# The list scheduler's second pass run a second time, on its own result

## The chip, the cores and the metric

The kernel runs on one core of one Trainium2 chip. The metric is the device time of one execution in microseconds (us), from the first instruction to the last with what the runtime puts around them. TensorE, VectorE, ScalarE, GpSimd and SyncE are called PE, DVE, ACT, POOL and SP in the profile. All compute engines take their own list of instructions in order; SP's list is the queue that starts nearly all transfers.

## What is computed

One layer on a sequence of 1024 tokens, width 2048, all in float32. One input projection feeds a sparse attention (an indexer picks 256 keys for each query) and a Mamba-2 mixer; one output projection joins them, and a layer norm closes the layer.

```python
u = einsum('bsd,de->bse', x, w_in)
q, k, v, z_attn, q_idx, k_idx, w_idx, z_ssd, xbc, dt_raw = split(u)
# attention: rope on q, k, q_idx, k_idx; 8 query heads on 2 kv heads
score = sum_h relu(q_idx . k_idx) * w_idx      # admissible chunks only
sel = top_k(score, 256)
o_attn = softmax(q . k[sel]) @ v[sel] * silu(z_attn)
# mixer: causal conv, then a scan over chunks of 64 tokens
y = ssd(silu(conv(xbc)), softplus(dt_raw + bias), a_log) + d_skip * xs
o_ssd = rms_norm_by_group(y * silu(z_ssd)) * norm_w
out = layer_norm(alpha * x + concat(o_attn, o_ssd) @ w_out)
```

## The kernel before, in words

**Arithmetic.** A float32 product is made of three products of rounded halves: high·high, high·low, low·high. So every raw block of weights (wr, 128 x 1024) is rounded to its high part by ScalarE (wh) and the remainder is taken by VectorE (wl); inputs have halves xh and xl in the same way. The projections are done with a scheme of fewer block products, for which sums of weight blocks are formed first (wr<-wr,wr, mostly on VectorE, t_wacc in line 1264) and results are stored to and reloaded from scratch arrays in memory (u2, u3, t2, p1 and the like). PSUM banks are called pj (four, for projections), a (three) and o (one). A bank is drained by VectorE (u<-pj,u, t_comb in line 1118: add a scratch tile and store it in u). Some banks are preloaded by ScalarE before their matmuls (pj<-u, t_base in line 1097), with a tile u that SP loads from memory.

**Stages.** In order of time: the opening loads (to 14 us), the projections mixed with the indexer, the two top-k searches (ScalarE counts with u<-s,sm, VectorE steps in sm), the attention, and the mixer (t_ssd in line 2442: eight s<-s,ac and an exp s<-s for each piece, and softplus and exp that need another ScalarE table), up to 1374 us; then the rest of the output projection to 1566 us, and the layer norm's tail. t_turn (line 2337) transposes blocks by four SP transfers u<-u.

**Where the order comes from.** kernel() (line 2845) has the order made in three steps. First, Layer.run() writes a draft: each call of an engine is recorded as an Item by Engine (line 340), placed by a greedy simulation. Second, Order (line 370) takes the list of items and makes a new list. Third, Program.emit (line 603) issues the list; that is why every instruction of the profile has line 626.

Order works thus. link (line 397) finds for each item the earlier items that it depends on, by the list's order on each buffer and region, so the uses of a buffer keep their sequence. blocks (line 433) joins successive full matmuls of the list, as long as no newer result from outside is needed, into blocks that stay together. deadlines (line 466) goes through the list and gives each TensorE item as its due time the sum of the busy times of the TensorE items **ahead of it in the list**; then, backwards, each other item must be due early enough for those that need it:

```python
if x.key == "PE":
    x.due = t
    t += x.busy
...
took = self.transfer(x) + self.landing(x) + x.busy if x.dma else x.took
for j in x.after:
    y = self.items[j]
    x.due = min(x.due, y.due - took - self.gap(x, y))
```

A transfer counts its modelled length and its landing, with LATE = 2500 ns on top. run (line 529) then simulates the engines: TensorE takes the first block **in the list's order**, among the next 100, whose inputs have been there for 500 ns (next_block, line 512), or else the one that is ready soonest; each of the other queues takes, of the items that are ready, the one with the earliest due time. Eight lanes stand for transfers under way, and a change of ScalarE's table costs 1283 ns. The result is sorted by simulated start. Both the due times and TensorE's preference thus hang on the order of the list that comes in. In the kernel before, that is the draft's.

The function that the change touches:

## Time and profile before

| | |
|---|---|
| time, median of 3 runs | 1579.01 us (1578.07 to 1580.04) |
| the profiled execution's own time | 1579.93 us |
| its span, first to last instruction | 1578.1 us |
| granted TensorE clock | 0.997 |
| busy: PE / PEld / DVE / ACT / POOL | 1557.7 / 1302.0 / 1348.1 / 1026.3 / 221.9 us |
| transfers | 442.36 MB; queue q1 81.7% of 16 engines' span |

PE is TensorE's matmuls, PEld its loading of weights, which runs beside them. Names in the profile are those of tiles without their numbers: "pj<-xh,wh" is a matmul into a projection bank, "DMA wr<-wt" a load of raw weights. An idle time is given in brackets with what ended it. All instructions have line 626, so the tile names tell the step.

### The profile page before, as it was taken

Reading aid. Unit: us, or ns where it says so; the run is one execution under the profiler, and the core shown is the slowest. Engines: PE = TensorE matmul, PEld = TensorE weight load, DVE = VectorE, ACT = ScalarE, POOL = GpSimd, SP = SyncE. Lnnn points to the kernel's source line nnn. Section 1 sums busy time; section 2 is a strip of 40 time slices with the busy share of each in tenths; the row PEclk is TensorE's granted clock in tenths of the full one; section 3 lists DMA queues with packets and bytes.
Section 4 is the critical chain, followed back from the end, with each engine's and each line's share of the span. In section 5 each row is a group of like instructions: output and inputs, shape, how many; then the busy total and the mean of one; then the engine's idle time right before and its main releaser. Section 6 shows DMA issues by size and latency. Waiting matters only on the chain.

```text
span 1578.1 us, 24028 instructions
## 1 busy us (share of the span) xinstructions
PE 1557.7 (99%) x7677; PEld 1302.0 (82%) x7677; DVE 1348.1 (85%) x2499; ACT 1026.3 (65%) x1881; POOL 221.9 (14%) x219
## 2 busy tenths in 40 slices
PE   9999999999999999999999999999999999999997
PEld 7888898888888888888878888888878888788885
DVE  5989999997779897788968888997789777879996
ACT  5466676858996999777334575596877675733440
POOL 0000300011000010101312222163110002100200
PEclk9999999999999999999999999999999999999998
DMA  9558977899878886689879865877999999997653
GB/s 346 210 196 279 346 240 235 298 370 404 300 223 291 282 316 225 227 269 313 241 246 384 281 216 181 297 219 243 345 360 359 323 384 315 345 363 252 204 180 107
DMA packets 248766, 442.36 MB, mean 280 GB/s; under 512 B 52384, under 2 KB 107328, under 8 KB 248640
## 3 DMA queue, kind: packets, MB, share of 16 engines
q1 hardware_dynamic: 248128, 440.45, 81.7%
q8 instruction: 60, 0.98, 0.3%
q14 instruction: 66, 0.54, 0.1%
q10 hardware_dynamic: 512, 0.39, 0.1%
HBM read 319.23 MB, written 112.08 MB: 273 GB/s over the span
## 4 chain that ended last, share of the span: by engine, by line
PE 80%; DMA 10%; DVE 4%; SPq 3%; ACT 2%; issue 1%; POOL 0%; ACTq 0%; DVEq 0%; POOLq 0%
PE pj L626 64%; PE a L626 13%; PE o L626 3%; SPq L626 3%; DMA wr<-wt 2%; DVE u L626 2%; DMA zs<-u 1%; DMA u<-u 1%; DMA u<-o 1%; ACT s L626 1%; ACT u L626 1%; DMA u<-mx 1%; DVE wl L626 1%; DMA s<-arow 1%; DMA wr<-t 0%
## 5 line engine op out<-in xcount | busy, mean ns | idle before, releaser
L626 PE MATMUL pj<-xh,wh 128*128 128x512 f32 (+1 forms) x1496 | 576.9, 386 | 5.2 <-DVE u L626 3.2
L626 PE MATMUL pj<-xh,wl 128*128 128x512 f32 (+1 forms) x1496 | 570.2, 381 | 0.5 <-DVE wl L626 0.5
L626 PE MATMUL pj<-xl,wh 128*128 128x512 f32 (+1 forms) x1496 | 570.6, 382 | 0.0
L626 ACT ACTIVATE wh<-wr 128x1024 fp32r<-128x1024 f32 (+3 forms) x242 | 249.0, 1029 | 156.9 <-PE pj L626 115.2
L626 DVE TENSOR_TENSOR wl<-wr,wh 128x1024 fp32r<-128x1024 f32 (+3 forms) x239 | 293.1, 1227 | 46.1 <-ACT wh L626 42.7
L626 PEld LDWEIGHTS pj<-xh,wh 128*128 128x128 f32 x1496 | 281.6, 188 | 59.6 <-ACT pj L626 3.1
L626 PEld LDWEIGHTS pj<-xh,wl 128*128 128x128 f32 x1496 | 281.2, 188 | 55.1 <-DVE wl L626 1.3
L626 PEld LDWEIGHTS pj<-xl,wh 128*128 128x128 f32 x1496 | 281.6, 188 | 49.8 <-DVE xl L626 0.3
L626 DVE TENSOR_TENSOR u<-u,u 128x512 f32<-128x512 f32 (+8 forms) x242 | 157.4, 660 | 25.7 <-ACT u L626 14.6
L626 ACT ACTIVATE u<-u 128x512 f32<-128x512 f32 (+5 forms) x200 | 108.3, 553 | 104.3 <-DVE u L626 46.2
L626 PE MATMUL a<-u,u 128*128 128x512 f32 (+3 forms) x710 | 165.5, 343 | 0.7 <-DVE s L626 0.4
L626 PEld LDWEIGHTS a<-u,u 128*128 128x128 f32 x710 | 118.2, 189 | 20.8 <-DVE s L626 1.7
L626 ACT ACTIVATE u<-s,sm 128x896 bf16<-128x896 int16 (+7 forms) x132 | 129.0, 978 | 8.7 <-DVE sm L626 8.0
L626 PE MATMUL pj<-wh,xh 128*128 128x512 f32 x318 | 127.2, 401 | 0.0
L626 PE MATMUL pj<-wl,xh 128*128 128x512 f32 x318 | 124.3, 391 | 0.0
L626 PE MATMUL pj<-wh,xl 128*128 128x512 f32 x318 | 124.0, 391 | 0.0
L626 ACT ACTIVATE a<-a 128x512 f32<-128x512 f32 (+3 forms) x160 | 78.5, 504 | 58.2 <-PE a L626 50.1
L626 DVE TENSOR_TENSOR wr<-wr,wr 128x1024 f32<-128x1024 f32 (+1 forms) x78 | 95.9, 1231 | 8.4 <-DMA wr<-wt 5.8
L626 DVE TENSOR_TENSOR u<-pj,u 128x512 f32<-128x512 f32 (+1 forms) x109 | 72.2, 664 | 20.1 <-PE pj L626 18.2
L626 POOL TENSOR_SCALAR s<-s,sm 128x128 f32<-128x128 f32 (+7 forms) x64 | 64.0, 1013 | 135.8 <-DVE sm L626 116.4
L626 DVE SCALAR_TENSOR_TENSOR s<-a,wsc,s 128x512 f32<-128x512 f32 (+3 forms) x120 | 73.6, 644 | 4.5 <-ACT a L626 3.9
L626 DVE SCALAR_TENSOR_TENSOR u<-cv,cw,u 128x512 f32<-128x512 f32 x96 | 71.7, 762 | 2.4 <-ACT u L626 2.1
(289 smaller groups left out, 2161.7 us busy)
## 6 DMA issues: line engine op xcount, KB each, us to landing
wr<-wt SPq DMA_DIRECT2D x187, 512.0 KB, 5.5
u<-u SPq DMA_DIRECT2D x110, 256.0 KB, 5.2
wr<-t SPq DMA_DIRECT2D x44, 512.0 KB, 6.1
u<-wo SPq DMA_DIRECT2D x64, 256.0 KB, 4.1
ts<-u SPq DMA_DIRECT2D x64, 256.0 KB, 4.9
wr<-ts SPq DMA_DIRECT2D x32, 512.0 KB, 6.0
s<-xt SPq DMA_DIRECT2D x25, 512.0 KB, 6.4
wr<-wo SPq DMA_DIRECT2D x23, 512.0 KB, 6.2
```

The costliest lines, as they stand in the source:

```text
L626: getattr(engines[x.eng], x.op)(*[real(v) for v in x.args], **{k: real(v) for k, v in x.kw.items()})
```

## The change

The pass over the order is made twice: the second one takes the first one's result as its list. Nothing else is changed: the same items, costs, tiles and pools.

```diff
-        items = Order(layer.fl.sim, layer.fl.items).run()
+        items = layer.fl.items
+        for _ in range(2):
+            items = Order(layer.fl.sim, items).run()
```

In the second pass the due times are sums over the first pass's TensorE order, the blocks are cut from that order, and the preference of TensorE follows it. The set of instructions stays equal but for ScalarE's table loads (45, then 43). TensorE's order is the same up to about 30 us and from about 1374 us on; in between it differs in 44 pieces, and 1243 of 7427 steps change place. Three places:

SP's queue at 804 to 813 us, before. Names have a tile's number and that of its making; u_1514 is a transposing transfer (x4), wr_1501 and wr_1502 are the two weight blocks whose sum VectorE forms, u_1504 and u_1509 are scratch tiles, the u2, u3 and t2 are stores.

```order
L626 DMA u_1504_8525<-p1_1_6_6454 128x512
L626 DMA u3_1_4_8529<-u_1437_8057 128x512
L626 DMA u2_1_5_8537<-u_1484_8316 128x512
L626 DMA t2_1_6_8541<-wr_1433_8300 128x1024
L626 DMA u_1514_8550<-u_1513_8497 128x1x128 x4
L626 DMA wr_1501_8581<-wt 128x1024
L626 DMA wr_1502_8585<-wt 128x1024
L626 DMA u_1509_8591<-p1_1_7_6509 128x512
L626 DMA t2_1_7_8604<-wr_1463_8409 128x1024
L626 DMA u_1518_8609<-u_1517_8594 128x1x128 x4
```

The same place after:

```order
L626 DMA u_1504_8530<-p1_1_6_6444 128x512
L626 DMA u2_1_5_8539<-u_1484_8392 128x512
L626 DMA u_1498_8545<-u_1497_8438 128x1x128 x4
L626 DMA u3_1_4_8562<-u_1437_7950 128x512
L626 DMA wr_1501_8569<-wt 128x1024
L626 DMA wr_1502_8573<-wt 128x1024
L626 DMA u_1509_8580<-p1_1_7_6504 128x512
L626 DMA u_1514_8584<-u_1513_8535 128x1x128 x4
L626 DMA t2_1_7_8602<-wr_1463_8368 128x1024
L626 DMA wr_1503_8614<-wt 128x1024
L626 DMA u_1518_8624<-u_1517_8600 128x1x128 x4
```

The loads of wr_1501 and wr_1502 stand ahead of u_1514's four transfers, and behind those of u_1498; wr_1503 comes ahead of u_1518; t2_1_6 stands earlier, before this piece.

SP's queue at 1139 to 1147 us, before. u_2281 is the tile with which ScalarE preloads a bank; u_2259 to u_2261 feed the mixer's gate; wr_2275 and wr_2274 are weight blocks, mx a store.

```order
L626 DMA wr_2253_12276<-t2_1_5_8199 128x1024
L626 DMA u_2175_12298<-c0_3_10399 128x2x256
L626 DMA wr_2275_12304<-wt 128x1024
L626 DMA u_2259_12311<-z0_6_12231 128x512
L626 DMA u_2260_12319<-o0_3_11522 128x512
L626 DMA u_2281_12324<-u3_1_2_8185 128x512
L626 DMA u_2261_12335<-o0_3_11522 128x512
L626 DMA mx1_7_12344<-u_2188_11861 128x512
L626 DMA wr_2274_12353<-t2_1_6_8541 128x1024
```

After:

```order
L626 DMA wr_2253_12264<-t2_1_5_8189 128x1024
L626 DMA s4_2202_12281<-arow0_2758 128x2x512
L626 DMA u_2175_12287<-c0_3_10399 128x2x256
L626 DMA mx1_7_12295<-u_2188_11869 128x512
L626 DMA wr_2274_12305<-t2_1_6_8378 128x1024
L626 DMA u_2281_12310<-u3_1_2_8183 128x512
L626 DMA u_2259_12314<-z0_6_12243 128x512
L626 DMA u_2260_12328<-o0_3_11455 128x512
L626 DMA u_2261_12339<-o0_3_11455 128x512
L626 DMA wr_2275_12352<-wt 128x1024
```

u_2281 now stands ahead of u_2259, u_2260 and wr_2275, and behind mx1_7 and wr_2274. On ScalarE its preload goes ahead of all eight steps s<-s,ac of that piece instead of behind six of them.

ScalarE's queue at 1202 to 1211 us, before. pj_2397<-u_2394 preloads a bank; s4_2266 are the mixer's eight steps and its exp (128x1024); xh_2379 and xh_2366 are rounded inputs; u_2271 a product with a piece's row.

```order
L626 ACTIVATE xh_2379_12887<-u_2360_12819 128x512
L626 ACT_TABLE_LOAD
L626 ACTIVATE u_2271_12486<-s4_2266_12650 64x512
L626 ACTIVATE wh_2391_12910<-wr_2343_12740 128x1024
L626 ACTIVATE u_2271_12486<-s4_2266_12650 64x512
L626 ACTIVATE s4_2266_12650<-s4_2266_12650,ac1_933 128x128 x3
L626 ACTIVATE xh_2366_12941<-u_2357_12868 128x512
L626 ACTIVATE s4_2266_12650<-s4_2266_12650,ac1_933 128x128 x3
L626 ACTIVATE pj_2397_12960<-u_2394_12884 128x512
L626 ACTIVATE s4_2266_12650<-s4_2266_12650,ac1_933 128x128 x2
L626 ACTIVATE s4_2368_12572,sm_2414_12976<-a_2415_12969,eps_130 128x128 x2
L626 ACTIVATE s4_2266_12650<-s4_2266_12650 128x1024
```

After:

```order
L626 ACTIVATE xh_2362_12860<-u_2356_12780 128x512
L626 ACT_TABLE_LOAD
L626 ACTIVATE u_2271_12491<-s4_2266_12575 64x512 x2
L626 ACTIVATE wh_2391_12898<-wr_2343_12731 128x1024
L626 ACTIVATE s4_2266_12575<-s4_2266_12575,ac1_935 128x128 x7
L626 ACTIVATE xh_2366_12935<-u_2357_12866 128x512
L626 ACTIVATE s4_2266_12575<-s4_2266_12575,ac1_935 128x128
L626 ACTIVATE xh_2379_12944<-u_2360_12834 128x512
L626 ACTIVATE s4_2266_12575<-s4_2266_12575 128x1024
L626 ACTIVATE pj_2397_12966<-u_2394_12882 128x512
```

The preload of pj_2397 stands behind all eight steps, xh_2379 and the exp; xh_2379 stands behind xh_2366 instead of ahead of the table load.

## The prediction, made blind

> **What bounds the kernel now.** I read the engine totals first, then TensorE's busy time by stretch, then the list of its waits, and last the timeline around the largest of them. The totals of the page and the engine line of its chain of waits:
>
> ```profile
> PE 1557.7 (99%) x7677; PEld 1302.0 (82%) x7677; DVE 1348.1 (85%) x2499; ACT 1026.3 (65%) x1881; POOL 221.9 (14%) x219
> PE 80%; DMA 10%; DVE 4%; SPq 3%; ACT 2%; issue 1%; POOL 0%; ACTq 0%; DVEq 0%; POOLq 0%
> ```
>
> TensorE's busy time in four stretches; the columns are the stretch, its length, PE busy (instructions), granted clock, DMA share and GB/s:
>
> ```profile
> 0.00:14.00 14.00, 12.38 (x42) 1.00 0.78 246
> 14.00:1374.00 1360.00, 1352.23 (x6771) 1.00 0.84 289
> 1374.00:1566.00 192.00, 192.00 (x864) 1.00 0.69 232
> 1566.00:1578.10 12.10, 1.10 (x5) 0.64 0.49 141
> ```
>
> TensorE stands still for 1578.1 − 1557.71 = 20.4 us: 1.6 in the opening, 7.77 in the long middle, 0 in the output projection, 11.0 in the tail. The change leaves all work and its engines as they are, so it can win only idle time of TensorE. Its two orders are equal for TensorE up to about 30 us and from about 1374 us on, so opening, output projection and tail keep theirs: **at most 7.8 us (and what restarting costs) are to be had, all in the middle.** Nothing of the kind bounds a loss. Who ended the waits (us in total, times, longest):
>
> ```profile
> PE pj L626 <- DVE u L626: 3.2, 2, 1.9
> PE pj L626 <- ACT pj L626: 1.7, 2, 0.9
> PE o L626 <- DVE s L626: 0.6, 1, 0.6
> PE o L626 <- PE a L626: 0.5, 1, 0.5
> ```
>
> Six waits hold 6.0 of the 7.77 us. In the timeline of TensorE (start, length, instruction, idle before it):
>
> ```profile
> 721.40 0.47 PE L626 MATMUL pj<-xh,wh 128*128 128x512 f32 x1 [1.31 <-DVE u L626]
> 818.63 0.50 PE L626 MATMUL pj<-xh,wh 128*128 128x512 f32 x1 [1.87 <-DVE u L626]
> 1133.33 0.86 PE L626 MATMUL o<-s,u 128*128 128x256 f32 x5 [0.58 <-DVE s L626]
> 1153.92 0.50 PE L626 MATMUL pj<-xh,wh 128*128 128x512 f32 x1 [0.86 <-ACT pj L626]
> 1209.49 0.50 PE L626 MATMUL pj<-xh,wh 128*128 128x512 f32 x1 [0.89 <-ACT pj L626]
> 1351.81 1.09 PE L626 MATMUL o<-s,u 128*64 128x128 f32 x16 [0.51 <-PE a L626]
> ```
>
> Everywhere else TensorE takes up its next matmul without a gap, so a step of VectorE, ScalarE or a transfer that moves there costs nothing as long as it lands within the slack that the row of matmuls ahead gives it. The sum is therefore made over these six places, and then over the places that may become new ones.
>
> **The change part by part.** Counts of matmuls, vector instructions and transfers stay equal; the list falls from 45 to 43 ScalarE table loads. 1243 of the 7427 TensorE steps change place, by 77 at most, and so do 1575 of VectorE's 2379, 876 of ScalarE's 1546 and 738 of SP's 1468, mostly by one or two.
>
> *818.6 us.* SP's queue, then VectorE's, ahead of the longest wait:
>
> ```profile
> 806.54 4.04 SPq L626 DMA_DIRECT2D u<-u  x4
> 810.63 1.09 SPq L626 DMA_DIRECT2D wr<-wt  x2
> 813.09 0.69 DVE L626 TENSOR_TENSOR u<-u,u 128x512 fp32r<-128x512 f32 x1 [4.11 <-ACT u L626]
> 816.75 1.23 DVE L626 TENSOR_TENSOR wr<-wr,wr 128x1024 f32<-128x1024 f32 x1 [2.97 <-DMA wr<-wt]
> 817.89 1.28 DVE L626 TENSOR_TENSOR u<-pj,u 128x512 f32<-128x512 f32 x2
> ```
>
> The two weight loads stand behind four transpose transfers that hold SP for 4.04 us. VectorE then waits 2.97 us for them, sums them (1.23), and only then drains the PSUM bank (half of 1.28) that TensorE wants. In the new order those four transfers come behind the loads. Issued 4.0 us earlier, the loads have landed by about 812.7, when VectorE is free, and the drain no longer waits: −1.87. What was moved back, the four transfers, feeds a step of TensorE that itself stands 11 matmuls later. If u_1498's four, which now stand right ahead of the loads, hold them as long, 0.
>
> *721.4 us.* The last two of VectorE's steps before the wait ends:
>
> ```profile
> 719.43 1.22 DVE L626 TENSOR_TENSOR wl<-wr,wh 128x1024 fp32r<-128x1024 f32 x1
> 720.57 0.68 DVE L626 TENSOR_TENSOR u<-pj,u 128x512 f32<-128x512 f32 x1
> ```
>
> VectorE is working without a gap; the drain is late because it stands behind other work. The new order carries a weight sum into the piece ahead of the drain and small top-k steps out of it. A sum costs this much, if its data is there:
>
> ```profile
> L626 DVE TENSOR_TENSOR wr<-wr,wr 128x1024 f32<-128x1024 f32 x76 | 93.5, 1231 | 8.4 <-DMA wr<-wt 5.8 <-DMA wr<-t 2.5
> ```
>
> Bounds: −1.31 (wait gone), +0.8 (two thirds of a sum unhidden). I take −0.6, since several steps of the same size leave the piece.
>
> *1153.9 us.* TensorE waits for ScalarE's preload of a PSUM bank (pj<-u); ScalarE waits for that preload's own load, which SP issues last of these:
>
> ```profile
> 1143.36 0.32 SPq L626 DMA_DIRECT2D u<-z  x1
> 1144.41 0.32 SPq L626 DMA_DIRECT2D u<-o  x1
> 1144.79 0.42 SPq L626 DMA_DIRECT2D u<-u  x1
> 1153.27 0.60 ACT L626 ACTIVATE pj<-u 128x512 f32<-128x512 f32 x1 [1.03 <-DMA u<-u]
> ```
>
> Now that load precedes the u<-z and the two u<-o, and a weight load less and a store and another weight load more stand ahead of it; it can be issued about 1 us earlier. −0.86; 0 if DMA is too full (8.5 us pass here from issue to use).
>
> *1351.8 us.* A few hundred ns of VectorE work leave the chain that ends at it: −0.51, bound 0.
>
> *1209.5 us.* Another preload, with ScalarE's steps around it:
>
> ```profile
> 1202.36 0.63 ACT L626 ACTIVATE xh<-u 128x512 fp32r<-128x512 f32 x1 [1.35 <-DMA u<-mx]
> 1208.86 0.58 ACT L626 ACTIVATE pj<-u 128x512 f32<-128x512 f32 x1
> 1209.38 0.68 ACT L626 ACTIVATE s<-s,ac 128x128 f32<-128x128 f32 x2
> 1210.65 1.05 ACT L626 ACTIVATE s<-s 128x1024 f32<-128x1024 f32 x1
> ```
>
> The new order puts the preload behind the two small steps (0.68), the exp (1.05) and that xh (0.63): 2.36 later. The xh leaves its old place, with the 1.35 us that ScalarE waited there: 1.98 earlier. Net +0.4; bounds −0.3 (the earlier start counts, the exp moves past) and +2.0 (little of that start survives, as data of the steps between comes later).
>
> *1133.3 us.* A vector step s<-a,s that TensorE waits for:
>
> ```profile
> 1130.44 0.69 DVE L626 TENSOR_TENSOR u<-a,u 128x512 fp32r<-128x512 f32 x1 [2.26 <-DMA o<-u]
> 1132.58 0.69 DVE L626 TENSOR_TENSOR s<-a,s 128x512 fp32r<-128x512 f32 x1
> 1133.78 0.42 DVE L626 TENSOR_TENSOR u<-u,dt 128x256 f32<-128x256 f32 x1
> ```
>
> It goes behind the u<-u,dt (0.42) and a weight sum (1231 ns, the row above); part of the sum may fill the 2.26 us that VectorE stood still just before: +0.5, bounds −0.58 (wait gone) and +1.5 (nothing fills).
>
> Sum of the six: −1.87 − 0.6 − 0.86 − 0.51 + 0.4 + 0.5 = −2.9.
>
> *New waits.* Where 1243 matmul steps and their feeders trade places, TensorE will wait somewhere it does not now. No row prices that; the nearest is the old order's own yield, 7.77 us over 6771 matmuls. A new draw over the reordered sixth gives 7.77 × 1243/6771 = 1.4. Bounds: 0, and 3.7 (two waits like the longest). I take 1.4.
>
> *ScalarE's two table loads fewer.* At the mean of their row that frees 2 × 1.28 = 2.6 us of ScalarE, off the path:
>
> ```profile
> L626 ACT ACT_TABLE_LOAD x45 | 57.7, 1283 | 7.8 <-DVE sm L626 3.0 <-issue 2.9 <-DMA zs<-u 1.2
> ```
>
> **Net −2.9 + 1.4 = −1.5 us.** The profiled execution took 1579.93, its span 1578.1; 1.8 us lie around the span. Forecast of a like execution: 1578.4. The median of the three runs is 1579.01, 0.9 lower, so the forecast of the median is 1577.5.
>
> [...] The row first: a stretch in which TensorE waits for nobody (length, then busy time and instructions of PE, PEld, DVE, ACT and POOL, then clock and DMA):
>
> ```profile
> 1400.00:1500.00 100.00, 100.00 (x443) 82.81 (x442) 93.40 (x136) 35.57 (x45) 9.66 (x6) 1.00 0.75 252
> ```
>
> TensorE's weight loads (PEld) are busy for 82.81% there with TensorE without a gap, 226 ns a matmul. 1302.0 us of loads at that share make 1572.3 us, 5.8 under the span, much like the 7.77. [...]
>
> **The rivals.**
>
> (A) *Slower: steps are pulled forward whose data isn't there.* Each engine takes its list in order. Where the second pass lists a weight sum or an exp ahead of a PSUM drain or preload, and its data comes no earlier, VectorE or ScalarE stands still with the drain behind it. The places are the drain of 721 (a sum ahead of it, whose load moved eight places back), the step of 1133 and the preload of 1209. The row at 816.75 prices it: 2.97 us of standing still, 1.87 of them reaching TensorE. Three times that, 5.6, in the place of my terms for these three: −1.87 − 0.86 − 0.51 + 5.6 + 1.4 = +3.8, so 1582.8; with only two of them hit it is about +2 and no difference. For it: VectorE's sums already stand 8.4 us for transfers, and DMA is full where two of the places lie (its share is the last number but one):
>
> ```profile
> 1060.00:1170.00 110.00, 108.32 (x556) 1.00 0.93 303
> 1170.00:1374.00 204.00, 202.18 (x1067) 1.00 1.01 344
> ```
>
> Against it: the list holds every step back until its modelled load has landed. Chance 0.24.
>
> (B) *Faster by more: nearly all waits of the middle go.* Due times taken from an order nearer to the one that runs are more right at every place, so few new waits come. The six places at their sum and no new wait give −2.9, at their good ends −5.4, all 7.77 us at most: 1571.2 to 1575.8 beyond the 0.2%. For it: four of the six places gain in the order, two by moves that match the cause of their wait. Against: two lose by the same rule, and the modelled costs of transfers, which made these waits, stay as they are. Chance 0.30. Below 1571 would need matmuls closer than 226 ns, the room that the rule speaks of: 0.01 of the 0.30.
>
> (C) *The change doesn't do what it says.* Due times hardly alter what is late, as the waits come from durations of transfers that the model doesn't know. Then waits are only traded: 1578 to 1580. It lies within my forecast's class.
>
> **How the numbers follow.** 0.2% is 3.2 us, about what a measurement of this kernel can tell from no change. My forecast (−1.5, and its neighbours on both sides within 0.2%) has 0.36 and C 0.10, both inside; B 0.30 is faster; A 0.24 is slower, less 0.01 for the part of it that ends inside: 0.30, 0.47, 0.23. The range goes from 1572.5 (a net of −6.5: the good ends of the six, −1.87 − 1.31 − 0.86 − 0.51 − 0.3 − 0.58 = −5.4, and part of what the smaller waits hold) to 1583.5 (A, with 0.7 for the ends of its terms). The likeliest case alone, with no new wait or with 3.7 us of them, runs from −2.9 to +0.8: 1576.1 to 1579.8.
>
> **What would show it.** Right: PE busy of the middle at about 1353.7 of 1360 or a middle shorter by 1.5; no wait at the drain that stood at 818.6, and the weight sum before it with no idle; no wait on the preload at 1153.9; 43 table loads; larger waits at 1209 and 1133. Wrong: a wait of 2 us or more on VectorE's drain at a place that has none now (A), or hardly any wait over 0.3 us in the middle (B), or any difference in the output projection or the tail.

## The result, and the profile after

The changed kernel takes 1590.61 us (median of 3 runs, 1588.66 to 1591.55), against 1579.01: a ratio of 1.0069 with a 95% interval of 1.0055 to 1.0082, 11 us **slower**. The forecast was 1577.5, with a range that ended at 1583.5. The profiled execution has a span of 1588.8 us, 10.7 more than before.

Busy times of the page after, then TensorE by stretch as before (length, PE busy, granted clock, DMA share, GB/s); the middle's end has moved from 1374 to about 1384:

```profile
PE 1562.3 (98%) x7677; PEld 1303.4 (82%) x7677; DVE 1356.4 (85%) x2499; ACT 1021.8 (64%) x1879; POOL 234.0 (15%) x219
```

```profile
0.00:14.00 14.00, 12.17 (x42) 1.00 0.80 262
14.00:1384.00 1370.00, 1357.55 (x6772) 1.00 0.85 287
1384.00:1576.00 192.00, 190.88 (x860) 1.00 0.69 226
```

The middle has grown by 10 us; opening and output projection have not (the 1.1 us missing in the last row belong to the middle's last wait, at 1385). TensorE is busy for 4.6 us more with the same 7677 matmuls, and its idle time in the middle has risen from 7.8 to 12.5, or 13.6 with that last wait. Its waits (us in total, times, longest):

```profile
PE a L626 <- POOL sm L626: 3.0, 2, 1.8
PE pj L626 <- ACT pj L626: 2.5, 3, 1.0
PE pj L626 <- DVE u L626: 2.2, 3, 1.2
PE o L626 <- DVE s L626: 1.1, 1, 1.1
PE o L626 <- ACT u L626: 1.0, 2, 0.7
```

There is no large wait of the kind that rival A had in mind (the longest is 1.84), but there are many of about 1 us, one kind of them new (GpSimd's sm). To place the loss I compared the start of the same matmul in both traces where TensorE's order meets again. The lag is −0.05 us at 720, +1.2 at 752, **+8.2 at 814**, +5.9 at 827, +7.7 at 1240, **+9.9 at 1366**, +10.5 at 1376, and stays. Two pieces hold most of it: 752 to 814 (+7.1) and 1330 to 1376 (+2.7).

**The piece up to 814 us.** TensorE after, with idle times, and its windows:

```profile
811.55 0.88 PE L626 MATMUL pj<-u,u 128*128 128x256 f32 x5 [0.34 <-DVE u L626]
812.76 0.39 PE L626 MATMUL o<-u,u 128*128 128x256 f32 x1 [0.34 <-ACT u L626]
813.49 1.08 PE L626 MATMUL o<-u,u 128*128 128x256 f32 x5 [0.34 <-DVE u L626]
815.24 0.80 PE L626 MATMUL pj<-xh,wh 128*128 128x512 f32 x1 [0.68 <-DVE u L626]
815.84 0.63 PE L626 MATMUL pj<-xl,wh 128*128 128x512 f32 x1
816.26 0.63 PE L626 MATMUL pj<-xh,wl 128*128 128x512 f32 x1
```

```profile
810.00:813.00 3.00, 2.27 (x11) 1.00 0.58 122
813.00:814.00 1.00, 0.66 (x5) 0.98 1.01 352
814.00:815.00 1.00, 0.57 (x3) 0.50 0.82 231
815.00:821.00 6.00, 5.76 (x15) 0.52 0.93 294
```

Four short waits stand between and behind narrow matmuls that feed one another through VectorE and ScalarE. From 814.0 us on, ahead of the last of them, the granted clock is at half for about 7 us: a matmul of 512 columns starts every 427 ns (815.84, 816.26) instead of 227. Start to start, the waits between 802 and 815 cost 3.8 us and the halved clock 3.2. That is also where most of the greater busy time comes from: TensorE is "busy" for those 427 ns too.

Why those matmuls were fed late is seen on three queues. VectorE's last step of the second top-k search, before and after:

```profile
743.14 0.62 DVE L626 SCALAR_TENSOR_TENSOR u<-u,sm,u 128x384 f32<-128x384 f32 x1
```

```profile
758.92 0.62 DVE L626 SCALAR_TENSOR_TENSOR u<-u,sm,u 128x384 f32<-128x384 f32 x1
```

**The search ends 15.8 us later.** It is a chain: ScalarE counts, VectorE takes a few tiny steps, ScalarE counts again. From 705 to 760 us ScalarE waited for these steps, before and after:

```profile
ACT u L626 <- DVE sm L626: 4.0, 7, 1.1
```

```profile
ACT u L626 <- DVE sm L626: 11.6, 8, 2.8
```

At 705 to 708 us the search stood level in both traces; then its steps stood behind weight work in VectorE's list (for one, a wl of 1.22 us at 717.18 ahead of the step at 718.32, for which ScalarE waited 2.8 us). On SP the transposing transfers of the searched rows follow its end; before, and after:

```profile
744.50 2.49 SPq L626 DMA_DIRECT2D u<-u  x4
```

```profile
757.91 0.33 SPq L626 DMA_DIRECT2D wr<-wt  x1
758.34 0.39 SPq L626 DMA_DIRECT2D u<-wo  x1
762.88 0.33 SPq L626 DMA_DIRECT2D wr<-wt  x1
763.26 2.49 SPq L626 DMA_DIRECT2D u<-u  x4
...
795.71 14.72 SPq L626 DMA_DIRECT2D u<-u  x20
```

The first four start 18.8 us later, and SP, at 0.65 to 0.74 us for one, does not make all of that up: it issues 20 in a row until 810.4, and TensorE starves at 811. Between the two stands ScalarE, after:

```profile
810.14 0.63 ACT L626 ACTIVATE u<-u 128x512 fp32r<-128x512 f32 x1 [2.63 <-DMA u<-u]
```

It waits for a transposed block, VectorE for its result, and TensorE, at 811.55, for VectorE's.

**The piece up to 1376 us.** GpSimd's two power steps on 2 columns, before and after, and VectorE's work beside the second of them after:

```profile
1362.68 1.97 POOL L626 TENSOR_TENSOR sm<-sm,mhalf 128x2 f32<-128x2 f32 x2 [12.31 <-ACT u L626]
```

```profile
1370.54 4.98 POOL L626 TENSOR_TENSOR sm<-sm,mhalf 128x2 f32<-128x2 f32 x2 [12.35 <-ACT u L626]
```

```profile
1372.02 1.21 DVE L626 TENSOR_TENSOR wl<-wr,wh 128x1024 fp32r<-128x1024 f32 x1
1373.16 0.68 DVE L626 TENSOR_TENSOR xh<-xh,u 128x512 f32<-128x512 f32 x1
1373.76 1.21 DVE L626 TENSOR_TENSOR wl<-wr,wh 128x1024 fp32r<-128x1024 f32 x1
```

A step of about 1 us takes 3.7 here while VectorE streams pairs of SBUF tiles without a pause, and TensorE waits 1.8 us for it (and again at 1385).

### The profile page after: what moved, and what is told of

Its sections match the earlier page's. It is cut to its first block, busy times and chain, and to the rows that moved or that the text cites. A ratio compares the mean times of both kernels' runs of the same rounds, so it can differ in the third digit from the quotient of the medians.

```text
span 1588.8 us, 24030 instructions
## 1 busy us (share of the span) xinstructions
PE 1562.3 (98%) x7677; PEld 1303.4 (82%) x7677; DVE 1356.4 (85%) x2499; ACT 1021.8 (64%) x1879; POOL 234.0 (15%) x219
## 4 chain that ended last, share of the span: by engine, by line
PE 84%; DMA 7%; DVE 3%; ACT 2%; SPq 2%; issue 1%; POOL 1%; DVEq 0%; ACTq 0%; POOLq 0%
PE pj L626 68%; PE a L626 13%; PE o L626 3%; SPq L626 2%; DVE u L626 2%; DMA zs<-u 1%; DMA wr<-t 1%; DMA wr<-wt 1%; ACT u L626 1%; DMA u<-u 1%; DMA s<-arow 1%; DMA c<-u 1%; POOL sm L626 1%; DMA u<-wo 0%; DMA z<-u 0%
## 5 line engine op out<-in xcount | busy, mean ns | idle before, releaser
L626 DVE TENSOR_TENSOR wl<-wr,wh 128x1024 fp32r<-128x1024 f32 (+3 forms) x239 | 287.9, 1206 | 38.2 <-ACT wh L626 36.2
L626 DVE TENSOR_TENSOR u<-u,u 128x512 f32<-128x512 f32 (+7 forms) x242 | 155.6, 653 | 11.9 <-ACT u L626 5.7
L626 ACT ACTIVATE u<-s,sm 128x1024 bf16<-128x1024 f32 (+7 forms) x132 | 128.9, 978 | 12.3 <-DVE sm L626 11.8
L626 DVE TENSOR_TENSOR wr<-wr,wr 128x1024 f32<-128x1024 f32 (+1 forms) x78 | 96.9, 1244 | 15.8 <-DMA wr<-wt 11.7
L626 POOL TENSOR_SCALAR s<-s,sm 128x640 f32<-128x640 f32 (+7 forms) x64 | 66.6, 1055 | 151.9 <-DVE sm L626 127.0
```

The lines of the kernel that those rows point to most:

```text
L626: getattr(engines[x.eng], x.op)(*[real(v) for v in x.args], **{k: real(v) for k, v in x.kw.items()})
```

## The experiments

The theory, **T**: the second pass takes its due times from an order in which the top-k search was already late. TensorE's first steps that need it stand later there, so the search is due later, while weight work is not. It loses its turn on VectorE, ends 16 us later, and its transposes crowd SP until TensorE starves. Rivals: **S**, two weight loads at the head of SP's queue hold the transposes (3.1 and 4.5 us from the issue before to theirs, at 757.91 and 762.88); **P**, TensorE's own new order bunches narrow matmuls, whatever the due times. **G** is the theory for the second piece, **C** one on the clock. Given the first pass's due times for every item, the second pass gives back the first pass's list, so that kernel is the one before.

The kernel's own lists bear out the first link of T. Of the search's 56 items that the first pass places behind 705 us, 52 are due 9.9 us later in the second pass, as is the first matmul that hangs on them; the ten weight sums and remainders (wr, wl) that it places on VectorE between 707 and 760 us are due at the same time as in the first or 0.7 us earlier.

**The search's due times alone undone** (e1).

```diff
+ first = Order(sim, draft); due = {x: x.due for x in draft}
+ items = first.run(); second = Order(sim, items)
+ for x in items:
+     if any(o.tensor.name.startswith(("sm_718_", "u_719_")) for o in x.outs):
+         x.due = min(x.due, due[x])
+ items = second.run()
```

> The changed kernel, but the counting steps of the second top-k search (ScalarE's u<-s,sm and VectorE's sm, one key of each pair) keep the due times of the first pass where these are earlier. Theory T (the search loses its priority to weight work, ends 16 us later, at 759 instead of 743 us, and its transposes then crowd SP's queue until TensorE starves at 811 to 815 us): the search ends at about 743 again, the piece from 752 to 814 us takes its old 62 us instead of 69, no halved clock there, and the time falls by 6 to 9 us from 1590.6, to 1581 to 1585, since the other new waits stay. Rival S (two weight loads that head SP's queue hold the transposes for 2.7 and 4.2 us; when the search ends does not matter): 1588 to 1591. Rival P (TensorE's own new order bunches narrow matmuls, whatever the due times): 1588 to 1591.

1581.95 us, ratio to before 1.0019 (1.0006 to 1.0031). The search ends at 741.4, and the clock stays whole:

```profile
741.43 0.61 DVE L626 SCALAR_TENSOR_TENSOR u<-u,sm,u 128x384 f32<-128x384 f32 x1
```

```profile
810.00:815.00 5.00, 5.00 (x26) 1.00 1.00 320
815.00:821.00 6.00, 5.00 (x24) 1.00 0.75 248
```

The piece 752 to 814 loses nothing more (the lag stays at 1.2), and by the ratios about 8 of the 11 us are gone; the 3 that remain are the second piece, where the lag grows from 0.9 to 3.7. T holds; S and P alone do not explain it, for TensorE's list is still the first pass's result.

**The search made late in the kernel before** (e2): one pass, `x.due += 10000.0` for the same items.

> The kernel before with one pass, and the same counting steps of the top-k search made due 10 us later, nothing else touched. T: the loss of the changed kernel appears with this alone: search ends 10 to 17 us later, TensorE starves at about 810, time 1585 to 1590. S: the weight loads keep their due times, so at most 2 us over 1579. P: TensorE's list is the draft's, so 1578 to 1581.

1588.23 us, ratio 1.0054 (1.0038 to 1.007). The search ends at 759.0, TensorE lags by 9.1 us more over 752 to 814, and a wait of 3.73 us for VectorE's drain ends at 828, with a halved clock from 827 on (0.50 from 828 to 832). One cause alone, put into the old kernel, gives a loss of nearly the whole size. The places are not all those that T named: the first waits are for rounded weights (1.93 us at 769.12 for ScalarE's wh, 0.86 at 772.11 for VectorE's wl, with a halved clock of 3.4 us, 0.61 and 0.54 in the 2 us from 772 and from 774), and the burst at 811 comes as one at 815 to 817. That the late search costs this much is shown; that it must do so through SP is not.

**SP's due times undone** (e3): `if x.eng == "SP": x.due = due[x]` in place of the condition above.

> The changed kernel with the due times of SP's transfers alone taken from the first pass, so that weight loads and transposes stand against each other as before. S: most of the 7 us goes, 1582 to 1584. T: the search still ends at about 750 or later, so most of the loss stays, 1586 to 1591. P: 1588 to 1591.

1589.83 us, ratio 1.0063 (1.0043 to 1.0084). The search still ends at 749.4. S falls as the main cause.

**The two loads moved behind the transposes** (e11), in the changed kernel's list.

```diff
+ held = [loads of wr_1433 and wr_1462]
+ items = [x for x in items if x not in held]
+ items[n + 1:n + 1] = held      # n: last transfer of u_1415
```

> The changed kernel with two weight loads (wr_1433, wr_1462) moved in SP's queue from ahead of the first twelve transposing transfers to right behind them; nothing else is moved. S: the loads held the transposes, so most of the 7 us between 752 and 814 goes: 1583 to 1586. T: the transposes can start at 759.6, when the search ends, instead of 763.3, 16 us later than before the change still, so at most 2 us are won: 1588 to 1591.

1591.46 us, ratio 1.0073 (1.0056 to 1.0091). The transposes do start earlier:

```profile
759.34 2.49 SPq L626 DMA_DIRECT2D u<-u  x4
```

They start at the search's end, no sooner. The lag gained from 752 to 814 is only 3.0 us instead of 7.1, but it grows by another 3 up to 833, with a halved clock at 822 to 829 (0.53 on average): the loss moved, and the sum did not. S is a part of the path and not its length.

**All due times of the second pass, with the draft's list** (e4), from which TensorE's blocks and preference come.

```diff
+ items = Order(sim, draft).run(); second = Order(sim, items)
+ due = {x: x.due for x in items}
+ third = Order(sim, draft)
+ for x in draft: x.due = due[x]
+ items = third.run()
```

> The draft's list, from which TensorE takes its blocks and its preference, with the due times of the second pass for all items. T: the due times carry the loss, 1585 to 1590. S: the same, as SP's due times are among them. P: the loss comes with TensorE's list, so 1578 to 1581 here.

1584.00 us, ratio 1.0028 (1.0012 to 1.0044), between the two forecasts. The search ends as late as 756.5, yet the piece to 814 loses 3.0 us, not 7.1, and the clock stays whole there (1.00 in every 2 us from 752 to 814). So due times make the search late, and what the lateness costs depends on more than the lateness. TensorE's list doesn't settle it: e2 had the draft's list too, and there the late search cost 9.1 us over the same piece. The two differ chiefly in the due times of the other items; which of these make the difference is not shown. P is not borne out as a cause: e1 kept TensorE's new list and lost nothing here.

**Three passes** (e6).

> Three passes, each on the result of the one before. T: the due times drift later once more (the search again yields to weight work), so no gain over two passes: search ends at 755 or later, time 1587 to 1594. A rival (the second pass is an accident, a further one comes nearer to a settled order): 1579 to 1584.

1584.99 us, ratio 1.0045 (1.0033 to 1.0057): a miss for T's 1587 and for the rival's 1584. The search is late as foreseen (760.2), with a halved clock at 814 (0.50 from 814 to 816); the second piece lost nothing (its power steps took 0.9 and 0.8 us). TensorE's lag is 5.4 us at 839 (5.8 after two passes) and 6.9 at 1330 (7.7), then 6.4 at 1376 (10.5): the late search costs about the same, and the smaller loss is nearly all the second piece's.

**Each item due at the earlier of its two due times** (e5): `x.due = min(x.due, due[x])` for all.

> Two passes, but in the second each item is due at the earlier of its two due times. Theory T (lateness of the first pass that is written into the second's due times is what costs): no item loses its hurry, so search by 743, no halved clock, no stretched GpSimd step near 1365, and 1576 to 1580, level with the kernel before or up to 3 us under it. Rival P (a new order of TensorE costs by itself): 1583 or more.

1583.59 us, ratio 1.0032 (1.002 to 1.0044): not the 1576 to 1580. Its trace, of an execution of 1579.97 us, tells a part of it: TensorE is 3.0 us **ahead** of the kernel before at 1371, and loses it all in one wait:

```profile
PE a L626 <- POOL sm L626: 3.3, 1, 3.3
```

What the median of 1583.59 holds beyond that is not shown.

**The late items' due times undone as well** (e7): the search's items, and all that the first pass had due after 1300 us (`due[x] > 1300000.0`), get `x.due = due[x]`.

> The kernel of the run with the search's old due times, and besides all items that the first pass held due after 1300 us keep that due time. Theory G (the 2.7 us lost between 1340 and 1376 are GpSimd's two-element power steps, 3.7 and 3.5 us instead of 1.0 and 2.5 us, as VectorE now streams two-input work without a pause beside them): the steps take 1.0 and 2.5 us again, and the time falls by 2 to 3.5 us from 1582.0, to 1578.5 to 1580. Rival: the loss there has another cause (the transposes come later by themselves): 1581 to 1583.

1583.06 us, ratio 1.0033 (1.002 to 1.0046): not the 1578.5 to 1580. The first two power steps were short again (1.3 and 1.0 us), but the third, 2.47 us long in the kernel before, took 5.48, as in e5, and TensorE stood for it:

```profile
1367.35 5.48 POOL L626 TENSOR_TENSOR sm<-sm,mhalf 128x2 f32<-128x2 f32 x1 [4.67 <-ACT u L626]
```

```profile
1368.06 1.21 DVE L626 TENSOR_TENSOR wl<-wr,wh 128x1024 fp32r<-128x1024 f32 x1
1369.19 0.68 DVE L626 TENSOR_TENSOR xl<-xl,xh 128x512 fp32r<-128x512 f32 x1
...
1371.00 1.28 DVE L626 TENSOR_TENSOR u<-u,u 128x512 f32<-128x512 f32 x2
1372.20 0.41 DVE L626 TENSOR_TENSOR xh<-a,c 128x256 f32<-128x256 f32 x1
```

The step ends at 1372.83, 0.6 us after the start of VectorE's first instruction for 5 us with one operand in PSUM (xh<-a,c). That is a sharper form of G.

**That one instruction moved** (e9 on e7, e10 on e5): xh<-a,c goes right behind wl<-wr,wh.

```diff
+ x = next(VectorE item xh_2721 <- a, c)
+ items.remove(x)
+ items.insert(1 + index of VectorE's wl_2743, x)
```

> The run before with the search's and the late items' old due times, and one VectorE instruction moved in the list: the product of a PSUM tile with a constant (xh<-a,c, 128x256) now stands right behind wl<-wr,wh at 1369 us, ahead of five products of two SBUF tiles each, as in the kernel before the change. Theory G (GpSimd's step gets through only when VectorE does not read two SBUF tiles): the step of 5.48 us ends within 1 us of that instruction, at 2 to 3 us length, TensorE's wait of 3.3 us shrinks to under 1, no halved clock at 1374, and the time falls by 2.5 to 5 us from 1583, to 1578 to 1580.5. Rival (GpSimd's step waits for something else, its data or its own queue): 1582 to 1584.

> The run with the earlier of the two due times for each item, and the same one instruction moved. G: TensorE's wait of 3.3 us at 1372 goes, so 2.5 to 3.5 us less than without the move; since its trace stood 3.0 us ahead of the kernel before at 1371 us, a time 0 to 3 us under the kernel before. Rival: no change against the run without the move.

e9: 1581.13 us, ratio 1.0005 (0.9993 to 1.0017). e10: 1579.37 us, ratio 0.9998 (0.9984 to 1.0012). GpSimd and VectorE in e10:

```profile
1367.99 2.47 POOL L626 TENSOR_TENSOR sm<-sm,mhalf 128x2 f32<-128x2 f32 x1 [5.59 <-ACT u L626]
```

```profile
1369.83 0.41 DVE L626 TENSOR_TENSOR xh<-a,c 128x256 f32<-128x256 f32 x1
```

The step ends at 1370.46, again 0.6 us after xh<-a,c starts; it is 2.47 long, to the digit as in the kernel before, and the wait is gone. G holds for this step. By the ratios, each good to about 2 us, the move wins 4.4 us from e7 to e9 and 5.4 from e5 to e10, for a wait of 3.3; e9's median stayed 0.6 above its 1578 to 1580.5.

In e7 the step of 5.48 us went on past eight of VectorE's instructions on pairs of SBUF tiles that started after it. But the rows show another end of a step than the one beside an operand in PSUM, so the "only" of e9's theory is not borne out. In the changed kernel both steps of the second piece end 0.6 us after the start of an instruction of another kind (at 1371.86 and 1375.52), though all its tiles are in SBUF:

```profile
1371.23 0.86 DVE L626 SCALAR_TENSOR_TENSOR u<-u,dn,xh 128x256 f32<-128x256 f32 x2
1374.89 0.86 DVE L626 SCALAR_TENSOR_TENSOR u<-u,dn,u 128x256 f32<-128x256 f32 x2
```

Nor does each instruction of this kind bring the end: in e4 a step of 3.35 us at 1397.67 went on past two of them. So not every instruction with two SBUF inputs held the step up, and which do is not settled here.

With both causes undone the second pass is level with the kernel before; its trace (span 1576.4) is 1.7 us shorter, within what the runs scatter.

**TensorE's waits of the burst filled** (e8): the changed kernel, with one matmul of the group repeated 5, 5, 5 and 6 times in the four waits. The sum that these feed is changed.

> The changed kernel with 21 more matmuls (128x256, one of the six that stand there, repeated) put into TensorE's four waits between 811 and 815 us; they add products to a sum of the attention, which is thereby changed. Theory C (the waits in this burst make the clock fall to half for 7 us, 3.2 us of loss): the granted clock stays at 1.00 there and the time falls by 2 to 3.5 us, to 1587 to 1588.5, though work was added. Rival (the clock falls for another reason, or its fall costs nothing since TensorE would wait anyway): 1590 to 1593.

1589.34 us, ratio 1.007 (1.0057 to 1.0083), against 1.0069 without them. The clock did stay whole:

```profile
810.00:815.00 5.00, 5.00 (x35) 1.00 0.68 170
815.00:821.00 6.00, 5.08 (x23) 1.00 0.98 332
821.00:826.00 5.00, 4.00 (x20) 1.00 0.98 311
```

Against the trace without the fill TensorE gains 2.1 us up to 820, but 1.5 us are lost again at once, with a wait of 1.20 us for VectorE's drain at 822 that the changed kernel does not have, as TensorE comes there later. C holds for the clock and fails for the time: the 3.2 us of halved clock were not 3.2 us of the result.

## Why the prediction was wrong

*What bounds it.* "It can win only idle time" and "at most 7.8" held, and that nothing of the kind bounds a loss.

*818.6.* −1.87 foreseen; the lag falls by 1.8 there. The number came by luck, for the step behind it failed. VectorE's weight sum was to find its loads landed; after the change it waits for them nearly as long as before (2.78 us, before 2.97):

```profile
821.37 1.22 DVE L626 TENSOR_TENSOR wr<-wr,wr 128x1024 f32<-128x1024 f32 x1 [2.78 <-DMA wr<-wt]
```

The two loads are issued at 815.39 instead of 810.63, behind u_1498's four transfers and two stores, which is the case that the prediction priced at 0. TensorE doesn't wait for the drain because it comes to it only at 824.12, 5.5 us late; in e8, where its clock stays whole, a wait of 1.20 us stands there again.

*721.4.* −0.6 foreseen, for "several steps of the same size leave the piece". They left it, and the idle time still grew: two waits, of 0.96 us for ScalarE's s and 1.22 for VectorE's drain, stand where one of 1.31 stood, and the lag rises by 1.2. What I counted as relief, top-k steps carried out of the piece, was the harm: they were the search being put behind other work.

*1153.9 and 1351.8.* −0.86 and −0.51 foreseen, −0.4 and 0 measured; and the next preload behind the first of them, at 1167.1, now keeps TensorE waiting for 1.02 us instead of 0.12. *1209.5 and 1133.3.* +0.4 and +0.5 foreseen; 1.00 instead of 0.89 us idle, and 1.07 instead of 0.58 (lag +0.5). The six together moved by about −0.4 instead of −2.9.

*New waits: the step that failed.* "A new draw over the reordered sixth gives 1.4", bounds 0 and 3.7. Measured, everything beyond the six places is 10.7 + 0.4 = 11 us. None of the three signs that were to show the forecast wrong appeared. The step priced new waits as a fresh draw of the same kind, as if the second order were as good as the first and only different. It is not: the due times move one way. Where the first pass let a chain run late, the second takes that lateness as leave (9.9 us for the search; undone alone in e1, about 8 of the 11 us go). Nor did the sum have a term for the clock: the halved stretch at 814 lengthened the matmuls themselves by 3.2 us. I followed each place that waits now, and not the longest chain of small steps (the search, 705 to 743 us), whose end feeds 60 us of SP's queue.

*Rival A* had the sign and the kind of mechanism, work pulled ahead of a step that TensorE needs, but not the place: it looked for large waits at 721, 1133 and 1209. *B* had the reason backwards: due times taken from an order nearer to the one that runs are less right, not more, since they hold what went wrong. Its 0.01 for a time below 1571 stood on matmuls closer than 226 ns; for those of 512 columns no run shows that: where TensorE waits for nobody, from 1412 to 1512 us after the change, it again takes 443 in 100.00 us. *Table loads:* 43, as foreseen; their worth was put at nothing and was not tried by itself.

What stays open: why a search that is equally late costs 3.0 us over the first piece in e4, 7.1 after the change and 9.1 in e2. All three end it between 756 and 759 us; they differ in the due times of the other items and in TensorE's list, and no run tells these apart.

## What to carry to other kernels

A due time must come from what the work needs, not from when it last ran: feeding a schedule its own result turns lateness into permission. When an order changes, follow the longest chain of small dependent steps through every queue first; the waits that exist now tell what can be won, and not what can be lost. Take the sum of waits with care where TensorE also slows down: in e8 the stretch at half clock went, a gap of 1.20 us at full clock came, and the time stayed (ratio 1.007, without the fill 1.0069).

## What the runs showed of the hardware

*A burst of short waits was followed by a halved clock.* In the changed kernel no gap from 810 us to the drop at 814.0 was longer than 0.34 us, and TensorE was idle for about 1.1 us of these 4 (0.73 of the first 3, 0.34 of the last); yet the clock fell. One gap of 1.87 us at 818 in the kernel before left it whole (1.00 from 810 to 825). In e8, with these waits filled, it stayed whole too (1.00 from 810 to 826). A wait of 3.3 us was followed by a halved clock in e7 and not in e5 (1.00 in every 2 us from 1370 to 1380). In e7:

```profile
1372.00:1374.00 2.00, 1.11 (x6) 0.98 1.00 223
1374.00:1377.00 3.00, 3.00 (x9) 0.50 1.02 378
```

The halved stretch lasts 3.4 us in e7 (1373.9 to 1377.3) and 6.8 after the change (814.0 to 820.8). Why one wait is followed by it and another of the same length is not, these runs do not show.

*Small steps of GpSimd and of VectorE took longer beside some of the other's work.* GpSimd's power step on 2 columns took 0.97 and 1.03 us at 1362.68 before the change, beside mixed work, and 5.48 in e7, beside unbroken pairs of SBUF tiles. Two of the search's VectorE steps on 2 columns, after the change, ran beside weight sums of GpSimd (2.36 us from 719.69, 3.33 from 750.36) and ended with them, at 722.1 and 753.7:

```profile
720.15 1.91 DVE L626 TENSOR_TENSOR sm<-sm 128x2 f32<-128x2 f32 x1 [0.55 <-ACT u L626]
...
752.18 1.52 DVE L626 TENSOR_TENSOR sm<-sm 128x2 f32<-128x2 f32 x1 [0.76 <-ACT u L626]
```

Before, none of VectorE's steps on 2 columns from 705 to 745 took more than 0.166 us, and none ran beside a weight sum of GpSimd, whose only one there lasted from 709.40 to 712.19.
